# A two-layer retention and state-space trunk on one core: a reserve ahead of transposes in TensorE's order, a longer planned time for running-sum transfers, and a sigmoid as ScalarE's warm-up

## The chip, the cores and the metric

The kernel runs on one core of one Trainium2 chip. The metric is the device time of one execution in microseconds (us). TensorE (PE; PEld is its weight load) multiplies, VectorE (DVE) and ScalarE (ACT) do elementwise work, GpSimd (POOL) does a few small powers and accumulating transfers, and SyncE (SP) issues nearly all transfers. Every engine works through its own instructions strictly in the order in which they are written, and waits where an operand is not there yet.

## The reference

Two layers of: RMS norm; one wide projection; a retention mixer of four heads with rotary queries and keys; a state-space mixer of four groups with a causal convolution; gates; an output projection; RMS norm; a SwiGLU FFN. Sequence 256 in two chunks of 128, width 1024, all in float32. The parts that matter here:

```python
def hybrid_mixer(h, w_in, ...):
    u = h @ w_in
    q, k, v, g_ret, z, xbc, dt, gate_ret, gate_ssd = jnp.split(u, ...)
    yr = retention(rotary(q), rotary(k) * RET_DK ** -0.5, v)
    yr = silu(g_ret) * (yr * rsqrt(mean(yr * yr) + EPS))
    o_ret = yr @ ret_out
    xs, bm, cm = jnp.split(silu(causal_dwconv(xbc, conv_w, conv_b)), ...)
    dtp = softplus(dt + dt_bias)
    ys = ssd_scan(xs * dtp, dtp * a, bm, cm) + d_skip * xs   # exp(acs_i - acs_j), acs = cumsum(dtp * a)
    ys = ys * silu(z);  ys = ys * rsqrt(mean over a group(ys * ys) + EPS) * ssd_norm_w
    o_ssd = ys @ ssd_out
    return (sigmoid(gate_ret) * o_ret + sigmoid(gate_ssd) * o_ssd) @ w_o

def swiglu(h, w_gate_up, w_down):
    gate, up = jnp.split(h @ w_gate_up, [D_FF], axis=-1)
    return (silu(gate) * up) @ w_down
```

## The kernel before

A matrix product is done in three passes in a reduced float32 format: each operand is split into a high part (ACT, line 498 for the weights: `wh`) and the rest (DVE, line 519: `wl`), and lines 535 to 537 multiply high by high, high by low and low by high. Lines 954, 955 and 957 are the same for products whose weights stand still in PE (`fm_job`). A weight tile of 512 KB (`raw`) is loaded by SP (line 480) into one of 4 buffers and split into one of 6 pairs of `wh`, `wl`.

Work runs in jobs, one per block of columns: in the mixer v, gr and bc, then q, k and xs by turns, then g with the rest of xs, the product with `ret_out`, z, the product with `ssd_out`, and `w_o`; then the FFN. What comes out of a job with the sequence in rows must be turned for the next product. `transposed` (line 623; the transposes are line 630) does so: it takes a PSUM buffer `tr` (there are two), four PE transposes against the identity `ident` (part of the tile `cst`) fill it, ACT copies the high part and DVE subtracts for the low part. It is used on the gated retention (`g_post`), the gated state-space output (`z_post`), the gated FFN halves (`up_post`), the norms (`Norm.half`) and the merged mixer output (`ssd_post`). `xs_post` has transposes of its own (line 1505): the convolved, silu'd `sT` is turned back to rows.

The order of every engine's instructions is made in Python when the kernel is built. `Flow` plays the whole program as streams of operations, each with an engine, a planned cost in ns and a priority; whenever an engine is free in this play, it takes the ready operation of the lowest priority number and writes its instruction. A stream that yields a number waits for so many ns of planned time: no instruction comes of it, but what follows is written later on its engine. A transfer is waited for by such a number too. `Flow._loads` adds 1283 to an ACT operation whose function needs another table than the last one, but only when a last one is known: `self.table` begins as `None`.

`ssd_chunk` builds the decay matrix of one group and chunk. SP brings running sums broadcast to all partitions (line 1570, `seg<-acs`, 512 KB, two buffers `seg`); then ACT does eight 128-column differences (line 1580), then one 1024-column Exp, DVE multiplies it by the scores (`cbm`), and PE multiplies (`yps`, line 1612; `ips`, line 1599). The play gives the transfer 1500 for its issue on SP and 2500 after it.

At the start, `warm` runs one tiny ACT operation (line 1956) so that a function table is loaded before the data is there.

Of the kernel before, what the change touches and what calls it, by code (L numbers as in the profile page):

```python
# [11 lines left out]
AF = mybir.ActivationFunctionType  # L12
# [180 lines left out]
def trunk_kernel(  # L193
# [5 lines left out]
    nc = tc.nc  # L199
    HB, RB, TAIL, WARM = 6, 4, 5, 2  # L200
    APART, LATE = (), 2500.0
    PR0, SLACK = 1.6, 2500.0
    BESIDE = (8, 10, 12, 14, 11, 11, 9, 24, 44)
    APARTS, SUMS_PR = {}, 3.5
# [73 lines left out]
    mhalf = cp.tile([P, 2], F32, tag="mhalf", name="mhalf")  # L278
    junk = cp.tile([P, 2], F32, tag="junk", name="junk")
# [340 lines left out]
            for _ in range(4):  # L620
                fl.release(bigS["C"])

    def transposed(src, n, dst, i, t, pr, plain=None):
        yield from dst.take(i)
        yield trS

        def emit():
            ps = new_tr()
            for j in range(n):
                nc.tensor.transpose(out=ps[:, j * P : (j + 1) * P], in_=src[:, j * P : (j + 1) * P], identity=ident)  # L630
            return ps[:, : n * P].rearrange("p (j t) -> p j t", j=n)

        v = yield pe(110 * n, pr, emit)
        dh, dl = (a[:, :n, t * P : (t + 1) * P] for a in dst.at(i)[:2])
        yield act(n * P, pr, dh, v, AF.Copy, psum=True)
        yield tt(n * P, pr, dl, v, dh.bitcast(F32), ALU.subtract)
        fl.set(dst.ready[i][t])
        if plain:
            yield sxS
            x = new_sx("plain")  # L640
            yield act(n * P, pr, x.rearrange("p (j t) -> p j t", j=n), v, AF.Copy, psum=True)
            fl.set(plain, x)
        fl.release(trS)
# [545 lines left out]
    def layer(l, mix, nxt, opening=None):  # L1189
# [300 lines left out]
        def xs_post(g, jj):  # L1490
            def post(ps, second, j):
                if jj == 0:
                    yield bigS["C"]
                    fl.set(xs_t[g], new_big("C", F32, (P, NT, 512)))
                xs = yield xs_t[g]
                yield sxS
                sT = new_sx("sT").rearrange("p (b t) -> p b t", b=2)
                yield from conv(ps, second, 4 * g + 2 * jj, sT, j)
                yield trS

                def emit():
                    tps = new_tr()
                    for t in range(NT):
                        for b in range(2):
                            nc.tensor.transpose(out=tps[:, (2 * t + b) * P : (2 * t + b + 1) * P],  # L1505
                                                in_=sT[:, b, t * P : (t + 1) * P], identity=ident)
                    return tps

                tps = yield pe(440, j, emit)
                yield act(512, j, xs[:, :, jj * 256 : (jj + 1) * 256], tps.rearrange("p (t c) -> p t c", t=NT),  # L1510
                          AF.Copy, psum=True)
                fl.release(sxS)
                fl.release(trS)
                fl.set(xs_ev[g][jj])
            return post
# [48 lines left out]
        def ssd_chunk(g, t, lp, pr, dtt, acs, dec, dr, prm, cb, xs, x0_ev):  # L1564

            yield segS

            def bring():
                sg = new_seg()
                nc.sync.dma_start(out=sg, in_=dr[t, g * HPG : (g + 1) * HPG, :].partition_broadcast(P))  # L1570
                return sg

            sg = yield Op("sp", 1500, bring, lp)
            yield 2500.0
            c0 = t * NH + g * HPG

            def differences():

                for i in range(HPG):
                    nc.scalar.activation(out=sg[:, i, :], in_=sg[:, i, :], func=AF.Relu, scale=-1.0,  # L1580
                                         bias=acs[:, c0 + i : c0 + i + 1])

            yield Op("act", HPG * (0.833 * P + 185), differences, lp)
            yield act(1024, lp, sg, sg, AF.Exp, scale=-1.0)
            yield tt(1024, lp, sg, sg, cb[:, 2 * t, :].unsqueeze(1).broadcast_to([P, HPG, P]), ALU.mult)
            yield sxS
            xdt = new_sx("xdt")
            yield tt(512, lp, h3(xdt), h3(xs[:, t, :]), hb(dtt, t * NH, g), ALU.mult)
            yield sxS
            tail = new_sx("tail")  # L1590
            dsb = prm[:, 2, g * HPG : (g + 1) * HPG].unsqueeze(2).broadcast_to([P, HPG, HD])
            yield tt(512, lp, h3(tail), h3(xs[:, t, :]), dsb, ALU.mult)
            if t == 1:
                x0 = yield x0_ev
                yield accS

                def inter():
                    ps = new_acc("ips")
                    nc.tensor.matmul(ps, lhsT=cb[:, 1, :], rhs=x0, start=True, stop=True)  # L1599
                    return ps  # L1600

                ips = yield pe(856, pr, inter)
                yield tt(512, lp, h3(x0), h3(ips), hb(dec, 0, g), ALU.mult)
                fl.release(accS)
                yield tt(512, lp, tail, tail, x0, ALU.add)
                fl.release(sxS)
            yield accS

            def intra():
                ps = new_acc("yps")  # L1610
                for i in range(HPG):
                    nc.tensor.matmul(ps[:, i * HD : (i + 1) * HD], lhsT=sg[:, i, :], rhs=xdt[:, i * HD : (i + 1) * HD],  # L1612
                                     start=True, stop=True)
                return ps

            yps = yield pe(1780, pr, intra)
            fl.release(segS)
            yield tt(512, lp, xs[:, t, :], yps, tail, ALU.add)
            fl.release(accS)
            fl.release(sxS)  # L1620
            if t == 0:
                yield tt(512, lp, h3(xdt), h3(xdt), hb(dec, NH, g), ALU.mult)
                fl.set(x0_ev, xdt)
            else:
                fl.release(sxS)
                fl.release(cbmS)
                fl.set(ys_ev[g])
# [9 lines left out]
        yr = Operand(RH, ["Y", "Y", "A", "A"])  # L1637

        def g_post(hd):
            def post(t, ps, j, sem):  # L1640
                yield silS
                sil = new_sil()
                yield act(512, j, sil, ps, AF.Silu, psum=sem is accS)
                fl.release(sem)
                yt, rs = yield ret_ev[hd]
                yield stt(512, j, sil, yt[:, t, :], rs[:, t : t + 1], sil, ALU.mult, ALU.mult)
                if t == 1:
                    fl.release(bigS["A"])
                yield from transposed(sil, 4, yr, hd, t, j)
                fl.release(silS)  # L1650
            return post

# [15 lines left out]
        yz = Operand(SG, ["Y", "Y", "C", "C"])  # L1668
# [8 lines left out]
        def z_post(g):  # L1677
            def post(t, ps, j, sem):
                yield silS
                sil = new_sil()  # L1680
                yield act(512, j, sil, ps, AF.Silu, psum=sem is accS)
                fl.release(sem)
                yield ys_ev[g]
                y = xs_t[g].value[:, t, :]
                yield tt(512, j, sil, sil, y, ALU.mult)
                ss, ms = small2("ss"), small2("ms")
                yield act(512, j, y, sil, AF.Square, accum_out=ss[:, :1])
                if t == 1:
                    fl.release(bigS["C"])
                yield ts(1, j, ms[:, :1], ss[:, :1], 1.0 / 512, EPS, ALU.mult, ALU.add)  # L1690
                rz = yield from power(ms, 1, j, "rz", 6)
                w = yield wbs[g // 2]
                yield stt(512, j, sil, sil, rz[:, :1], w[:, (g % 2) * 512 : (g % 2 + 1) * 512], ALU.mult, ALU.mult)
                wb_left[g // 2] -= 1
                if not wb_left[g // 2]:
                    fl.release(wbS)
                yield from transposed(sil, 4, yz, g, t, j)
                fl.release(silS)
            return post

# [92 lines left out]
        def up_post(sg_ev, c):  # L1793
            def post(t, ps, j, sem):
                s = yield sg_ev[t]
                yield tt(512, j, s, ps, s, ALU.mult)
                fl.release(sem)
                yield from transposed(s, 4, gu, c, t, j)
                fl.release(silS)
            return post  # L1800

# [113 lines left out]
    def whole():  # L1915
# [37 lines left out]
        yield dve(8, -2, fills)  # L1953

        def warm():
            yield Op("act", 1400, lambda: nc.scalar.activation(out=junk, in_=mhalf, func=AF.Copy), -3)

        fl.spawn(warm())
        fl.spawn(warm_pe())
# [102 lines left out]
```

## Time and profile before

| what | us |
|---|---|
| median of 3 runs (1268.36 to 1273.1) | 1272.93 |
| the profiled execution | 1270.24 |
| its span, first to last instruction | 1268.4 |
| PE busy | 1254.4 |
| DVE busy | 1016.1 |
| ACT busy | 831.9 |
| granted TensorE clock, mean | 0.999 |

All times in rows are from the span's start. Matmuls are pipelined, so two that follow each other overlap: what one costs is read from the distance between two starts, not from its length. A stall of PE is the distance between two starts beyond what the same pair takes where nothing is late. Rows in brackets show idle time and who ended it.

### The profile page before, as it was taken

The page shows a single profiled execution, that of the slowest core. Times are in us where ns is not written, and L with a number is a line of the kernel's source. Part 1 is how long each engine was busy: PE and PEld are TensorE (multiplying, and loading weights), DVE is VectorE, ACT ScalarE, POOL GpSimd, SP SyncE. Part 2 cuts the span into 40 slices and gives each one's busy share as a digit, 9 for nine tenths or more (in the row PEclk, how much of TensorE's full clock was granted, in tenths as well). Part 3 has the DMA queues.
Part 4 walks back from the last instruction along what each step waited for, and adds up shares of the span by engine and source line. Part 5 has one row for each costly group of instructions (what it writes and reads, how often), then busy time and mean ns, then how long its engine had stood idle before and what let it go on. Part 6 is the DMA issues. An engine that isn't in the chain of part 4 may idle for free.

```text
span 1268.4 us, 17450 instructions
## 1 busy us (share of the span) xinstructions
PE 1254.4 (99%) x6330; PEld 1059.5 (84%) x6330; DVE 1016.1 (80%) x1388; ACT 831.9 (66%) x1244; POOL 52.3 (4%) x76
## 2 busy tenths in 40 slices
PE   9999999999999999999999999999999999999997
PEld 7789888888888888888888898888788888788886
DVE  6998888878576678999788888878875756889996
ACT  6876786786365466776576676866854643766754
POOL 0000000000010001001000000000000000010010
PEclk9999999999999999999999999999999999999999
DMA  8668554555565457886676475555555564678863
GB/s 297 219 167 285 181 174 166 175 182 192 158 222 201 159 175 223 291 223 210 225 218 219 126 263 167 167 183 181 186 181 171 203 207 150 210 205 266 287 175 119
DMA packets 72455, 253.96 MB, mean 200 GB/s; under 512 B 8336, under 2 KB 8592, under 8 KB 72368
## 3 DMA queue, kind: packets, MB, share of 16 engines
q1 hardware_dynamic: 66832, 233.32, 54.4%
q0 software_dynamic: 5248, 18.99, 7.7%
q8 instruction: 50, 0.82, 0.3%
q10 hardware_dynamic: 288, 0.52, 0.1%
q14 instruction: 37, 0.30, 0.1%
HBM read 251.69 MB, written 1.11 MB: 199 GB/s over the span
## 4 chain that ended last, share of the span: by engine, by line
PE 87%; ACT 5%; DMA 3%; DVE 2%; issue 2%; SPq 0%; POOLq 0%; POOL 0%; ACTq 0%
PE acc L535 19%; PE acc L536 19%; PE acc L537 19%; PE acc L954 13%; PE acc L955 8%; PE tr L630 2%; PE yps L1612 2%; PE acc L957 2%; ACT wh L498 1%; DMA seg<-acs 1%; DVE wl L519 1%; DMA raw<-in_w_tm_dram 1%; ACT seg L1580 1%; PE ips L1599 1%; PE tr L1505 1%
## 5 line engine op out<-in xcount | busy, mean ns | idle before, releaser
L519 DVE TENSOR_TENSOR wl<-raw,wh 128x1024 fp32r<-128x1024 f32 (+2 forms) x400 | 474.9, 1197 | 124.1 <-ACT wh L498 122.5
L498 ACT ACTIVATE wh<-raw 128x1024 fp32r<-128x1024 f32 (+2 forms) x400 | 409.1, 1036 | 207.4 <-PE acc L537 106.4
L954 PE MATMUL acc<-xT,wh 128*128 128x512 f32 x840 | 304.8, 400 | 0.0
L955 PE MATMUL acc<-xT,wl 128*128 128x256 f32 x960 | 250.8, 281 | 0.0
L535 PE MATMUL acc<-wh,xT 128*128 128x512 f32 (+1 forms) x568 | 219.7, 387 | 0.0
L537 PE MATMUL acc<-wh,xT 128*128 128x512 f32 (+1 forms) x568 | 216.3, 381 | 0.0
L536 PE MATMUL acc<-wl,xT 128*128 128x512 f32 (+1 forms) x568 | 216.2, 381 | 0.0
L955 PEld LDWEIGHTS acc<-xT,wl 128*128 128x128 f32 x960 | 181.6, 189 | 10.3
L954 PEld LDWEIGHTS acc<-xT,wh 128*128 128x128 f32 x840 | 158.1, 188 | 31.7
L537 PEld LDWEIGHTS acc<-wh,xT 128*128 128x128 f32 x568 | 106.7, 188 | 19.5
L536 PEld LDWEIGHTS acc<-wl,xT 128*128 128x128 f32 x568 | 106.8, 188 | 19.4 <-issue 0.5
L535 PEld LDWEIGHTS acc<-wh,xT 128*128 128x128 f32 x568 | 106.8, 188 | 18.9 <-issue 0.9
L498 ACT ACTIVATE wh<-raws 128x1024 fp32r<-128x1024 f32 x64 | 67.3, 1057 | 30.6 <-DVE raws L227 14.9
L519 DVE TENSOR_TENSOR wl<-raws,wh 128x1024 fp32r<-128x1024 f32 x64 | 77.3, 1221 | 8.7 <-ACT wh L498 7.9
L535 PE MATMUL acc<-wh,A 128*128 128x512 f32 x192 | 76.4, 398 | 0.0
L230 DVE SCALAR_TENSOR_TENSOR cc<-cc,cv 128x255 f32<-128x255 f32 (+1 forms) x144 | 68.4, 479 | 9.4 <-ACT cc L220 8.5
L537 PE MATMUL acc<-wh,A 128*128 128x512 f32 x192 | 74.9, 390 | 0.0
L536 PE MATMUL acc<-wl,A 128*128 128x512 f32 x192 | 74.8, 390 | 0.0
L535 PE MATMUL acc<-wh,C 128*128 128x512 f32 (+1 forms) x184 | 72.3, 393 | 0.0
L536 PE MATMUL acc<-wl,C 128*128 128x512 f32 (+1 forms) x184 | 71.1, 387 | 0.3
L537 PE MATMUL acc<-wh,C 128*128 128x512 f32 (+1 forms) x184 | 70.8, 385 | 0.0
L535 PE MATMUL acc<-wh,Y 128*128 128x512 f32 x160 | 64.5, 403 | 0.0
(176 smaller groups left out, 1850.4 us busy)
## 6 DMA issues: line engine op xcount, KB each, us to landing
raw<-in_w_tm_dram SPq DMA_DIRECT2D x104, 512.0 KB, 4.3
raw<-in_w_fm_dram SPq DMA_DIRECT2D x80, 512.0 KB, 4.2
raw<-in_w_gf_dram SPq DMA_DIRECT2D x40, 512.0 KB, 4.8
raw<-in_ret_out_dram SPq DMA_DIRECT2D x32, 512.0 KB, 4.1
raw<-in_ssd_out_dram SPq DMA_DIRECT2D x32, 512.0 KB, 3.3
raw<-in_w_gate_up_dram SPq DMA_DIRECT2D x32, 512.0 KB, 5.1
raw<-in_w_down_dram SPq DMA_DIRECT2D x28, 512.0 KB, 4.3
raw<-in_w_gr_dram SPq DMA_DIRECT2D x24, 352.0 KB, 4.1
```

Source lines behind the costliest of these rows:

```text
L230: return Op("dve", 1.04 * n + 130, lambda: nc.vector.scalar_tensor_tensor(out=out, in0=in0, scalar=scalar, in1=in1, op0=op0, op1=op1), pr)
L498: nc.scalar.activation(out=wh[:, :m], in_=raw[:, :m], func=AF.Copy)
L519: nc.vector.tensor_tensor(out=wl[:, :m], in0=raw[:, :m], in1=wh[:, :m].bitcast(F32), op=ALU.subtract)
L535: nc.tensor.matmul(ps, lhsT=lh, rhs=rh, start=first, stop=False, **kw)
L536: nc.tensor.matmul(ps, lhsT=lh, rhs=rl, start=False, stop=False, **kw)
L537: nc.tensor.matmul(ps, lhsT=ll, rhs=rh, start=False, stop=last, **kw)
L630: nc.tensor.transpose(out=ps[:, j * P : (j + 1) * P], in_=src[:, j * P : (j + 1) * P], identity=ident)
L954: nc.tensor.matmul(a, lhsT=wh[:, k % 4, fsl], rhs=x[:, k % 4, :, :], start=k == 0, stop=False)
L955: nc.tensor.matmul(a[:, :SEQ], lhsT=wl[:, k % 4, fsl], rhs=xh[:, k % 4, :], start=False, stop=False)
L957: nc.tensor.matmul(a, lhsT=wh[:, k % 4, fsl], rhs=x[:, k % 4, :, :], start=False, stop=True)
L1505: nc.tensor.transpose(out=tps[:, (2 * t + b) * P : (2 * t + b + 1) * P], in_=sT[:, b, t * P : (t + 1) * P], identity=ident)
L1612: nc.tensor.matmul(ps[:, i * HD : (i + 1) * HD], lhsT=sg[:, i, :], rhs=xdt[:, i * HD : (i + 1) * HD], start=True, stop=True)
```

## The change

Four things are written anew. `transposed` takes a `slack`: having got its PSUM buffer, the stream waits that long in planned time before its transposes become ready; `g_post`, `z_post` and `up_post` pass 1500, the norms and `ssd_post` pass none. `xs_post` waits 1500 likewise. The planned time behind the issue of a running-sum transfer goes from 2500 to 5000, so 6500 with the issue. The warm-up operation is a Sigmoid instead of a Copy, and the play is told so, so the first table is known to it. Nothing that is computed changes, and each engine has the same instructions but for table loads. Lines of the changed kernel stand 1 to 4 further down (498 is 499, 630 is 633, 1505 is 1509, 1580 is 1584).

```diff
+    SLOW = 1500.0
...
-    def transposed(src, n, dst, i, t, pr, plain=None):
+    def transposed(src, n, dst, i, t, pr, plain=None, slack=0.0):
         yield from dst.take(i)
         yield trS
+        if slack:
+            yield slack
...
                 yield from conv(ps, second, 4 * g + 2 * jj, sT, j)
                 yield trS
+                yield SLOW
...
             sg = yield Op("sp", 1500, bring, lp)
-            yield 2500.0
+            yield 5000.0
...
-                yield from transposed(sil, 4, yr, hd, t, j)
+                yield from transposed(sil, 4, yr, hd, t, j, slack=SLOW)
...
-                yield from transposed(sil, 4, yz, g, t, j)
+                yield from transposed(sil, 4, yz, g, t, j, slack=SLOW)
...
-                yield from transposed(s, 4, gu, c, t, j)
+                yield from transposed(s, 4, gu, c, t, j, slack=SLOW)
...
-            yield Op("act", 1400, lambda: nc.scalar.activation(out=junk, in_=mhalf, func=AF.Copy), -3)
+            yield Op("act", 1400, lambda: nc.scalar.activation(out=junk, in_=mhalf, func=AF.Sigmoid), -3, "sigmoid")
```

Three places show what this does to the order. First, ACT in the opening of layer 0: `D<-acc,rstd` is the first sigmoid (of the gate columns), `sil,ss<-h` the sum of squares of half a row of x, `xT` and `plain` what the transposes leave. Before:

```order
L498 ACTIVATE wh<-raw 128x1024
L220 ACT_TABLE_LOAD
L220 ACTIVATE D<-acc,rstd 128x320
L220 ACTIVATE xT<-tr 128x4x128
L498 ACTIVATE wh<-raw 128x1024
L220 ACTIVATE plain<-tr 128x512 x2
L498 ACTIVATE wh<-raw 128x1024
L220 ACTIVATE sil,ss<-h_79 128x512
```

and in the change:

```order
L499 ACTIVATE wh<-raw 128x1024
L221 ACTIVATE D<-acc,rstd 128x320
L221 ACTIVATE xT<-tr 128x4x128
L499 ACTIVATE wh<-raw 128x1024
L221 ACTIVATE plain<-tr 128x512 x2
L499 ACTIVATE wh<-raw 128x1024
L221 ACTIVATE sil,ss<-h_79 128x512
```

The table load is gone; the rest stands as it stood. Over the whole program ACT has 33 table loads before and 34 in the change: this one fewer and, in the mixer of layer 0 and elsewhere, two more.

Second, ACT in layer 1, where group 2's running sums are used while xs of group 3 is convolved: `seg<-seg,acs` are the differences, `seg<-seg` the Exp, `sT<-cc` the silu whose result PE then transposes. Before, from the table load for the Exp to that silu:

```order
L220 ACT_TABLE_LOAD
L220 ACTIVATE seg<-seg 128x1024
L220 ACTIVATE cc<-acc 128x256
L220 ACTIVATE cc<-cc,cv 128x256
L498 ACTIVATE wh<-raw 128x1024 x2
L220 ACTIVATE cc<-cc,cv 128x256
L498 ACTIVATE wh<-raw 128x1024
L220 ACTIVATE seg<-seg 128x1024
L220 ACTIVATE cc<-acc 128x256
L498 ACTIVATE wh<-raw 128x1024
L220 ACT_TABLE_LOAD
L220 ACTIVATE sT<-cc 128x512
```

and in the change, from the second set of differences:

```order
L1584 ACTIVATE seg<-seg,acs 128x128 x8
L221 ACTIVATE sT<-cc 128x512
L221 ACTIVATE cc<-cc,cv 128x256
L499 ACTIVATE wh<-raw 128x1024 x3
L221 ACTIVATE C<-tr 128x2x256
L221 ACTIVATE cc<-acc 128x256
L221 ACT_TABLE_LOAD
L221 ACTIVATE seg<-seg 128x1024
```

The silu now stands before both Exp operations and needs no table load of its own; on PE the four transposes of its result moved 24 matmuls towards the front.

Third, PE in layer 1's FFN, at the transposes of the first gated pair. Before, both halves stand together:

```order
L954 MATMUL acc<-xT,wh 128x512
L955 MATMUL acc<-xT,wl 128x256
L630 MATMUL tr<-cst,sil 128x128 x8
L954 MATMUL acc<-xT,wh 128x512
L955 MATMUL acc<-xT,wl 128x256
L954 MATMUL acc<-xT,wh 128x512
L955 MATMUL acc<-xT,wl 128x256
L954 MATMUL acc<-xT,wh 128x512
L955 MATMUL acc<-xT,wl 128x256 x2
L957 MATMUL acc<-xT,wh 128x512
```

and in the change:

```order
L957 MATMUL acc<-xT,wh 128x512
L958 MATMUL acc<-xT,wl 128x256
L957 MATMUL acc<-xT,wh 128x512
L958 MATMUL acc<-xT,wl 128x256
L957 MATMUL acc<-xT,wh 128x512
L958 MATMUL acc<-xT,wl 128x256
L633 MATMUL tr<-cst,sil 128x128 x4
L958 MATMUL acc<-xT,wl 128x256
L960 MATMUL acc<-xT,wh 128x512
L633 MATMUL tr<-cst,sil 128x128 x4
```

The first four stand three pairs of matmuls later (the three pairs that came right behind them before), the second four two matmuls behind those. Outside the mixers of both layers, such shifts are all that changes on PE; inside them, from the second xs transposes to the product with `ret_out`, retention products, transposes and `yps`, `ips` change places.

## The prediction

> **What bounds the kernel now.** I read the page first, then the waits of PE, then the timeline and the chain of waits around each place where PE stood still. The page's busy times, and PE's waits (us in all, times, longest):
>
> ```profile
> PE 1254.4 (99%) x6330; PEld 1059.5 (84%) x6330; DVE 1016.1 (80%) x1388; ACT 831.9 (66%) x1244; POOL 52.3 (4%) x76
> ```
>
> ```profile
> PE tr L1505 <- ACT sT L220: 2.8, 3, 1.6
> PE tr L630 <- DVE sil L230: 1.4, 1, 1.4
> PE idle L1945 <- DVE mhalf L1922: 1.3, 1, 1.3
> PE tr L630 <- DVE sil L227: 1.1, 1, 1.1
> ```
>
> PE is the bound, and there is little idle time to win: four kinds of wait, 6.6 us in all, half a per cent of the span. Three of the four are transposes (L630, L1505) whose source ACT or DVE had not finished; the fourth is the start. PE works in order, so everything behind a transpose waits as well. No change of order can win much more than these; the question is how much of the transposes' part goes.
>
> The stalls, read as the distance between starts, in order of time. The group at 566 also gives what is normal: a 256-column pass (L955) holds PE for 0.12, a 512-column one for 0.23.
>
> ```profile
> 35.04 0.39 PE L537 MATMUL acc<-wh,C 128*128 128x512 f32 x1
> 36.86 0.63 PE L630 MATMUL tr<-cst,sil 128*128 128x128 f32 x4 [1.43 <-DVE sil L230]
> ...
> 282.59 0.39 PE L537 MATMUL acc<-wh,xT 128*128 128x512 f32 x1
> 283.92 0.33 PE L1505 MATMUL tr<-cst,sT 128*128 128x128 f32 x1 [0.94 <-ACT sT L220]
> ...
> 565.99 0.28 PE L955 MATMUL acc<-xT,wl 128*128 128x256 f32 x1
> 566.11 0.40 PE L954 MATMUL acc<-xT,wh 128*128 128x512 f32 x1
> 566.34 0.28 PE L955 MATMUL acc<-xT,wl 128*128 128x256 f32 x1
> 566.65 0.33 PE L630 MATMUL tr<-cst,sil 128*128 128x128 f32 x1
> ...
> 818.68 0.28 PE L955 MATMUL acc<-xT,wl 128*128 128x256 f32 x1
> 819.21 0.33 PE L1505 MATMUL tr<-cst,sT 128*128 128x128 f32 x1 [0.25 <-ACT sT L220]
> ...
> 908.02 0.39 PE L537 MATMUL acc<-wh,xT 128*128 128x512 f32 x1
> 909.98 0.44 PE L1505 MATMUL tr<-cst,sT 128*128 128x128 f32 x2 [1.56 <-ACT sT L220]
> ...
> 1105.95 0.28 PE L955 MATMUL acc<-xT,wl 128*128 128x256 f32 x1
> 1107.31 1.25 PE L630 MATMUL tr<-cst,sil 128*128 128x128 f32 x8 [1.08 <-DVE sil L227]
> ```
>
> So the stalls are 1.59 (at 35), 1.10 (at 283), 0.19 (566), 0.41 (819), 1.73 (909) and 1.24 (1107), together 6.26 us.
>
> **The change part by part.**
>
> *The sigmoid warm-up* takes a table load off ACT. The stall at 35 lies behind it. ACT's timeline, SP's, and from the page what a weight tile of that kind takes to land (median, us):
>
> ```profile
> 27.90 1.28 ACT L220 ACT_TABLE_LOAD   x1
> 29.19 0.53 ACT L220 ACTIVATE D<-acc,rstd 128x320 f32<-128x320 f32 x1
> ...
> 33.56 2.02 ACT L498 ACTIVATE wh<-raw 128x1024 fp32r<-128x1024 f32 x2
> ```
>
> ```profile
> 27.12 2.37 SPq L480 DMA_DIRECT2D raw<-in_w_fm_dram  x2
> ```
>
> ```profile
> raw<-in_w_fm_dram SPq DMA_DIRECT2D x80, 512.0 KB, 4.2
> ```
>
> From 27.90 on ACT has no idle row until these two `wh` are done; DVE's `wl` and then the `sil` that PE wants stand behind them. Without the load all of it moves up by 1.28. What could hold it is a weight tile that has not landed: the second `wh` began near 34.5 and would begin at 33.2; its tile is the second of the two issues, some 2 us after 27.12, so 29.2 + 4.2 = 33.4. So 1.0 to 1.28 is won, and I take 1.2; 0.3 to 0.4 of the stall stays. The operation at the start loads one table in both kernels, so nothing is paid there. [...]
>
> *The 6.5 us for the running sums* is behind the three stalls at L1505. The chain of waits ahead of the longest, and of the tile `seg` ACT's wait for these transfers (us, times) and their time from issue to landing:
>
> ```profile
> 884.24 6.38 DMA seg<-acs
> 890.64 2.46 ACT seg L1580 x8
> ...
> 909.29 0.64 ACT sT L220
> ```
>
> ```profile
>   DMA seg<-acs: 8.4, 6
> ...
> DMA to landing us min/median/max: 3.8/5.1/7.2
> ```
>
> The play allowed 4.0, the transfers took 5.1 in the median. ACT stood 8.4 us in 6 places, with all its later work behind it, and the silu `sT` was late for PE. At 6.5 planned, only a transfer near the longest, 7.2, is late, by 0.7, and the transposes have 1.5 in hand. In layer 1 the silu now even stands ahead of both Exps and two table loads (2 x 1.28), while its transposes moved up by 24 matmuls, 24 x 0.23 = 5.5 at most: the one about pays for the other, and what is left of the stall is ACT's lateness, which the longer plan takes away. I take all three as gone: 1.10 + 0.41 + 1.73 = 3.24. Bounds: 1.51, if the longest stays whole where its transposes moved up, and 3.24.
>
> *The reserve of 1.5 us* moves L630 back. At 1107 three pairs go ahead, 3 x (0.23 + 0.12) = 1.05, so 0.19 of 1.24 stays. The 0.19 at 566 goes, with eight more matmuls ahead of its transposes. Sum 1.24; lower bound 1.05.
>
> *What it costs.* The transposes' results come 1.5 later. Behind the last z group stands the product with `ssd_out`, which reads that group in its last five of 16 steps at the earliest; the eleven before are 11 x 12 passes of 0.23, 30 us of cover. Were it gone, each would cost its 1.5. Two `tr` buffers are held longer; nothing on PE is queued for them but other transposes. ACT gets two more table loads, 2.6 us, hidden by the 34% of the span in which it is idle; exposed, they would cost that.
>
> The order of both mixers is made anew, and a new order can have a late operand of its own. Nearest row, of the waits of PE's weight loads:
>
> ```profile
> PEld acc L536 <- DVE wl L519: 2.9, 7, 0.5
> ```
>
> Outside transposes lateness reaches 0.5 at a time, with one longest of 1.73 among the transposes. Between none (a new order may as well have fewer) and two of the longest, 3.5, I take 0.5, since with the reserve the same lateness must pass 1.5 before PE sees it.
>
> Sum: 1.2 + 3.24 + 1.24 - 0.5 = 5.2 us, bounds 0.1 (1.0 + 1.51 + 1.05 - 3.5) and 5.8 (1.28 + 3.24 + 1.24). The profiled execution, 1270.24 (its span and 1.84 around it), becomes 1265.0. It lies 2.7 below the median of the three runs; the middle of all four is 1271.6, and from there it is 1266.4. I say 1266.
>
> **The rivals.**
>
> *The waits move rather than go.* Each late operand comes back at another place of the new mixer order, and only the warm-up and the FFN's shift pay: 1.2 + 1.24 = 2.4, time 1269. For it: only the running sums get a longer plan, and the tiles of `raw`, which had their share in the 1107 stall, do not. Against it: no such wait above 0.5 shows at present outside transposes.
>
> *More than the sum.* The three runs spread over 4.7 us, and the profiled one is below their median. If the slower runs differ by later transfers, the same transposes catch it there, and a reserve of 1.5 takes that away too: 8 us from the median, 1265. For it: the spread is of the stalls' size. Against it: nothing shows where the slow runs lose.
>
> *Slower.* SP works in order, and the last two `seg` loads of a layer wait for a buffer that PE frees (L1612), with weight tiles queued behind them:
>
> ```profile
> SPq L1570 <- PE yps L1612: 7.8, 4, 3.3
> ```
>
> The longer plan puts `yps` later. A tile of `ret_out` feeds 12 passes, 2.7 us; 4 raw and 6 split tiles are 27 us of reserve at most. Say half is filled: the wait must go from 3.3 to over 13 before PE starves, and it costs what is beyond. At 20 in both layers that is 2 x 7 = 14, less 5.2: slower by 9, 1280. Against it: 3 tiles stand behind the last load as before, and the loads moved by a place or two.
>
> *The transfers land in time anyway.* [...] With transfers inside the old 4.0 the 3.24 falls away and 2.0 is left, 1270. The shortest of the 16 took 3.8 and ACT did wait 8.4, so this is as good as excluded.
>
> **How the numbers follow.** My forecast (4.3 to 6.3 won, 1265.3 to 1267.3 from the middle run): 0.60. Moved waits: 0.23. More than the sum: 0.13. Slower: 0.03. In time anyway: 0.01. The forecast alone ranges from 1263 to 1268, by the run that it is taken from; with the moved waits above and the larger gain below, 1261 to 1271 leaves out the slower case and the two ends. What a measurement here can tell from no change is about 0.5%, 6.4 us: faster by that means under 1266.6, from the median. That is two thirds of my forecast (0.40) and most of the larger gain (0.11), together 0.51; slower 0.03; within 0.46.
>
> **What would show it.** Right: no table load before the first sigmoid, and the third group of transposes at some 35.6 with an idle of 0.2; ACT's wait for `seg` under 2 us in all; PE's wait for `sT` gone; the FFN transposes of layer 1 with 0.2 or none. Wrong: new rows of PE or PEld waiting in the mixers, ACT still idle for `seg`, or a wait of SP for `yps` above 10. A span that falls by 5 while the runs' median does not move would mean that the runs differ by something outside these stalls.

## The result, and the profile after

The changed kernel takes 1262.91 us in the median of 6 runs (1261.89 to 1263.68); the kernel before, run beside it, 1273.01 (1268.36 to 1276.12). The ratio is 0.9924, with a 95% interval of 0.9902 to 0.9946: faster by 10.1 us, where 1266 had been said. A second set of 6 runs gave 1262.75 against 1273.07. The profiled execution took 1261.89, its span 1260.1, which is 8.3 less than the span before. The times of the runs also lie closer together: within 1.8 us, before within 7.8.

The page of the changed kernel, its busy times and the head of its chain of waits, and its list of PE's waits (us in all, times, longest), which has these two rows and no other:

```profile
PE 1251.6 (99%) x6330; PEld 1061.8 (84%) x6330; DVE 1017.9 (81%) x1388; ACT 832.7 (66%) x1245; POOL 52.6 (4%) x76
...
PE 95%; DVE 2%; DMA 1%; issue 1%; ACT 0%; POOLq 0%; POOL 0%; ACTq 0%
```

```profile
PE idle L1949 <- DVE mhalf L1926: 1.3, 1, 1.3
PE acc L537 <- DVE wl L520: 0.2, 1, 0.2
```

All waits of transposes are gone. PE's idle time, span less busy, fell from 14.0 to 8.5 us, and its busy time by 2.8 with the same 6330 instructions. The idle rows ahead of the six stalls were 5.26 of that, while the stalls, read from start to start, were 6.26: the last matmul ahead of a stall still runs for 0.16 (0.39 less 0.23), which counts as busy. That is 1.0 of the 2.8; the other 1.8 lies in small spacings that no row of waits shows, so the six stalls were not all that was late.

The three places in the order of the program. First the opening, on ACT and on PE:

```profile
26.51 1.05 ACT L499 ACTIVATE wh<-raw 128x1024 fp32r<-128x1024 f32 x1
27.46 0.51 ACT L221 ACTIVATE D<-acc,rstd 128x320 f32<-128x320 f32 x1
...
33.16 1.06 ACT L499 ACTIVATE wh<-raw 128x1024 fp32r<-128x1024 f32 x1 [0.27 <-DMA raw<-in_w_fm_dram]
```

```profile
34.68 0.39 PE L538 MATMUL acc<-wh,C 128*128 128x512 f32 x1
35.11 0.63 PE L633 MATMUL tr<-cst,sil 128*128 128x128 f32 x4
```

No table load ahead of the sigmoid; the second weight tile is now waited for, 0.27; the transposes start 0.43 behind the last pass instead of 0.23, a stall of 0.20 where there was 1.59. Second, layer 1, where the longest stall was (ACT, then PE):

```profile
893.08 2.45 ACT L1584 ACTIVATE seg<-seg,acs 128x128 f32<-128x128 f32 x8
895.43 0.62 ACT L221 ACTIVATE sT<-cc 128x512 f32<-128x512 f32 x1
```

```profile
897.82 0.39 PE L538 MATMUL acc<-wh,xT 128*128 128x512 f32 x1
898.05 0.60 PE L1509 MATMUL tr<-cst,sT 128*128 128x128 f32 x4
```

The differences start without a wait, the silu follows, and its result is there 2.0 us before PE comes for it (895.43 + 0.62 against 898.05). Before, the transposes started 0.05 behind the end of their silu, having waited for it. Third, the FFN of layer 1:

```profile
1100.30 0.28 PE L958 MATMUL acc<-xT,wl 128*128 128x256 f32 x1
1100.42 0.60 PE L633 MATMUL tr<-cst,sil 128*128 128x128 f32 x4
```

0.12 between the starts, which is what a 256-column pass holds PE for: no stall. ACT has no wait for `seg` left at all, and its transfers took 4.2/5.0/5.6 us (shortest, median, longest), all inside the planned 6.5.

### The profile page after: what moved, and what is told of

It is laid out like the page before. It is cut to its first block, busy times and chain, and to the rows that moved or that the text cites. A ratio compares the mean times of both kernels' runs of the same rounds, so it can differ in the third digit from the quotient of the medians.

```text
span 1260.1 us, 17460 instructions
## 1 busy us (share of the span) xinstructions
PE 1251.6 (99%) x6330; PEld 1061.8 (84%) x6330; DVE 1017.9 (81%) x1388; ACT 832.7 (66%) x1245; POOL 52.6 (4%) x76
## 4 chain that ended last, share of the span: by engine, by line
PE 95%; DVE 2%; DMA 1%; issue 1%; ACT 0%; POOLq 0%; POOL 0%; ACTq 0%
PE acc L536 20%; PE acc L537 20%; PE acc L538 20%; PE acc L957 16%; PE acc L958 9%; PE tr L633 2%; PE acc L960 2%; PE yps L1616 2%; DVE wl L520 1%; DMA raw<-in_w_dw_dram 1%; PE tr L1509 1%; PE acc L1376 1%; PE ips L1603 1%; PE idle L1949 0%; PE y L537 0%
```

## The experiments

Twelve experiments ran, in three sets that each had their own runs of the kernel before beside them (medians 1272.43, 1273.07 and 1272.44). Only the second, from "changed, again" to reserve_3000, also had the changed kernel beside it; for late_silu and reserve_all the difference to the changed kernel is taken from its first 1262.91, and is good to the 0.6 by which the medians of before differ. In the table "ACT for `seg`" is the time that ACT waited for the running sums in the profiled execution, and "L1505" the longest wait of PE for `sT` there.

| kernel | median (range), us | runs | ratio to before, 95% | ACT for `seg` | L1505 |
|---|---|---|---|---|---|
| before, again | 1272.71 (1270.48–1274.34) | 8 | 0.9996 [0.9982, 1.0010] | 9.6 | 2.5 |
| warm_only | 1272.45 (1268.84–1276.42) | 12 | 0.9998 [0.9983, 1.0013] | 10.5 | 1.9 |
| seg_only | 1267.48 (1266.11–1270.97) | 9 | 0.9956 [0.9942, 0.9971] | 0.2 | none |
| reserve_only | 1264.67 (1263.44–1266.44) | 6 | 0.9934 [0.9918, 0.9950] | 2.2 | none |
| xs_reserve_only | 1266.88 (1265.42–1268.24) | 8 | 0.9950 [0.9932, 0.9967] | 4.9 | none |
| l630_reserve_only | 1266.27 (1265.54–1267.24) | 7 | 0.9951 [0.9931, 0.9971] | 4.6 | 0.2 |
| changed, again | 1262.75 (1262.05–1263.70) | 6 | 0.9921 [0.9901, 0.9942] | none | none |
| no_warm | 1264.04 (1263.70–1265.32) | 6 | 0.9933 [0.9909, 0.9956] | none | none |
| no_seg | 1264.06 (1262.65–1264.42) | 6 | 0.9930 [0.9909, 0.9951] | 2.0 | none |
| reserve_3000 | 1262.90 (1262.56–1263.38) | 6 | 0.9922 [0.9902, 0.9943] | 2.0 | none |
| late_silu | 1268.22 (1266.51–1269.68) | 10 | 0.9964 [0.9949, 0.9979] | none | 3.2 |
| reserve_all | 1264.97 (1264.13–1265.73) | 6 | 0.9938 [0.9915, 0.9962] | none | none |

### The kernel before again: what differs between its runs

No edit; it gives a second trace of the same program.

> The kernel before, unchanged: a second profiled execution of it. Its six times so far spread from 1268.36 to 1276.12, those of the change from 1261.89 to 1263.68. Theory 'lateness at the transposes': where this execution is slower than the first profiled one (span 1268.4), the extra stands as longer PE waits at the same places (tr L1505 from ACT sT, tr L630 from DVE sil), 1 to 3 us each; where it is as fast, the places and sizes are those of the first profile within 0.3 us. Rival 'something else': a slower span with the same transposes' stalls, and the extra in matmul spacing, in the opening or in waits for weight tiles.

The median is that of before. ACT's waits for the running sums and PE's waits for the silu, of the first profiled execution (PE's two rows, 0.94 and 1.56, stand in the prediction):

```profile
264.59 2.46 ACT L1580 ACTIVATE seg<-seg,acs 128x128 f32<-128x128 f32 x8 [1.02 <-DMA seg<-acs]
890.64 2.46 ACT L1580 ACTIVATE seg<-seg,acs 128x128 f32<-128x128 f32 x8 [1.63 <-DMA seg<-acs]
```

and of the second, ACT and then PE:

```profile
266.18 2.45 ACT L1580 ACTIVATE seg<-seg,acs 128x128 f32<-128x128 f32 x8 [2.53 <-DMA seg<-acs]
893.88 2.46 ACT L1580 ACTIVATE seg<-seg,acs 128x128 f32<-128x128 f32 x8 [1.30 <-DMA seg<-acs]
```

```profile
282.68 0.39 PE L537 MATMUL acc<-wh,xT 128*128 128x512 f32 x1
285.51 0.87 PE L1505 MATMUL tr<-cst,sT 128*128 128x128 f32 x4 [2.45 <-ACT sT L220]
286.03 0.77 PE L535 MATMUL acc<-wh,xT 128*128 128x512 f32 x1
286.61 0.63 PE L536 MATMUL acc<-wl,xT 128*128 128x512 f32 x1
287.03 0.63 PE L537 MATMUL acc<-wh,xT 128*128 128x512 f32 x1
...
913.22 0.66 PE L1505 MATMUL tr<-cst,sT 128*128 128x128 f32 x4 [1.23 <-ACT sT L220]
```

ACT waits 1.02, 1.63, 2.53, 1.30; some 19 us later PE waits 0.94, 1.56, 2.45, 1.23. It is the same wait, handed on nearly whole: less 0.07 or 0.08 each time. Between the two ACT does not rest, so it cannot catch up. The windows of the first and of the second execution (length, then busy us of PE, PEld, DVE, ACT):

```profile
264.60:283.90 19.30, 18.38 (x94) 15.31 (x92) 14.08 (x23) 19.22 (x37) 0.00 (x0) 1.00 0.50 167
```

```profile
266.20:285.50 19.30, 16.86 (x85) 13.99 (x83) 13.85 (x22) 19.21 (x37) 0.00 (x0) 1.00 0.42 145
```

ACT is busy for 19.2 of 19.3 us there, although it is idle for a third of the span as a whole. ACT's other waits for `seg` did not reach PE like this: the longest of the first execution, 2.54 at 302, has no wait of PE behind it, and 0.70 at 799 came out as 0.25. So the time of a run of before depends on when a few of these transfers land. The first profiled execution had landed well at the first place (1.02); the second waited 2.53 there, and more followed: behind its stall passes start 0.43 apart instead of 0.23. Its windows around that place (the last columns are PEclk, DMA share, GB/s):

```profile
282.00:285.40 3.40, 1.06 (x5) 0.56 (x3) 3.40 (x5) 3.34 (x6) 0.00 (x0) 1.00 0.66 246
285.40:289.00 3.60, 3.49 (x11) 2.90 (x12) 3.59 (x6) 2.01 (x5) 0.00 (x0) 0.56 0.80 280
289.00:300.00 11.00, 11.00 (x63) 9.45 (x63) 9.41 (x12) 6.21 (x9) 0.00 (x0) 0.99 0.51 164
```

In the 3.6 us behind the stall the mean granted clock was 0.56. The eight passes there lose 8 x 0.20 = 1.6 on top of the 2.60 of the stall. The second span is 2.9 longer than the first (1271.3 against 1268.4), and this one place accounts for it: 1.50 more of stall, as the theory had it, and 1.6 in the spacing of matmuls, where the rival had looked. Other runs of before fit this: of the 57 beside the experiments, the 21 with a mean granted clock of 0.996 or 0.997 have a median of 1274.6, the 22 with 0.999 one of 1271.2.

### Each part alone: warm_only, seg_only, reserve_only

```diff
warm_only     AF.Copy  ->  AF.Sigmoid, ..., "sigmoid"      (L1956)
seg_only      yield 2500.0  ->  yield 5000.0               (L1574)
reserve_only  + yield SLOW in xs_post; slack=SLOW in g_post, z_post, up_post
```

> Only the warm-up operation is a sigmoid; the order of every engine stays as before but for one table load less on ACT. By the prediction's sum: 1.2 us less (1.0 to 1.28), the PE stall at 35 us falls from 1.6 to 0.3, all other stalls as before; times as widely spread as before's (over 4 us). [...] If the spread of the times came from the opening, it would fall here to under 2 us.

> Only the planned time of the running-sum transfers is 6.5 instead of 4.0 us; no reserve, warm-up as before. Prediction: ACT's wait for seg falls from 8.4 to under 2 us and the three stalls at L1505 (3.2 us) mostly go, the FFN stall of 1.2 and that at 35 (1.6) stay: 1.5 to 3.2 us less in the profile. Theory 'ACT's wait for the running sums makes the spread': the times spread under 2 us and the median falls by 6 or more. Theory 'zero reserve at the transposes makes the spread': they still spread over 3 us and the median falls by 1 to 4.

> Only the 1.5 us reserve ahead of the transposes of xs, gated retention, gated state-space output and FFN; running sums planned at 4.0 as before, warm-up as before. Prediction: ACT still waits some 8 us for seg, the FFN stall falls to 0.2, the L1505 stalls lose up to 1.5 each: 2.5 to 4 us less in the profile. Theory 'zero reserve makes the spread': the times spread under 2.5 us and the median falls by 6 or more. Theory 'ACT's wait makes the spread': spread over 3 us, median 2 to 4 less.

The warm-up alone wins nothing that shows in the median: the stall at 35 is gone from its trace (in an opening in which a weight tile had come late before it, so this trace does not decide whether the 0.3 expected would have been left), but the rest of the order is that of before, and its runs lie 7.6 us apart. Two of ACT's seven waits for `seg`, 1.95 and 1.93 of 10.5 us in all, came out as stalls of 2.04 and 2.01 at the same two places.

The longer plan alone wins 5.0, the reserve alone 7.8, more than the terms of 3.24 and 1.24 that they stood for. Together with nothing for the warm-up they would make 12.8, and the change won 10.1: seg_only and reserve_only take away the same stalls at L1505. Under the reserve ACT still waits 2.2 us for `seg`, but PE does not notice.

Neither theory of the spread came out whole. With the longer plan alone the runs still lie 4.9 apart, although no stall at L1505 is left: in its trace PE waits at L630, 1.5, 1.3 and 0.9 us. That trace is also of the slowest of its nine runs, with a span of 1269.1, 0.7 more than before where 1.5 to 3.2 less had been expected. With the reserve alone the runs lie 3.0 apart, closer to what "zero reserve makes the spread" had said (under 2.5), and the span is 3.7 less, as expected.

### Each part undone: no_warm, no_seg; and twice the reserve

```diff
no_warm       the changed kernel with  AF.Copy  for the warm-up
no_seg        the changed kernel with  yield 2500.0
reserve_3000  the changed kernel with  SLOW = 3000.0
```

> The changed kernel, unchanged, once more and beside the runs that leave one part out. 1262.9 with a spread of about 2 us, as before; the profile with no PE wait over 0.5 us behind the opening.

> The change without the sigmoid warm-up: one more table load on ACT ahead of the first sigmoid, every other instruction in the changed kernel's order. Alone, the warm-up moved the median by nothing (1272.45 against 1272.43, interval from -2.2 to +1.7 us), lost in the spread; here the spread is small. Prediction's term: 1.2 us slower than the changed kernel, with a stall of 1.3 to 1.6 at the third group of transposes (near 36 us). Rival, the opening is limited by transfers whatever ACT does: within 0.4 us of the changed kernel.

> The change with the running sums planned at 4.0 us as before. By the prediction's own terms the longer plan carried most of the three stalls: 2 to 3 us slower than the changed kernel, ACT waiting some 8 us for seg. Theory 'the reserve of 1.5 alone suffices': within 0.7 us of the changed kernel, ACT's wait for seg back at 8 us, and no PE wait behind it.

> The reserve at 3.0 instead of 1.5 us of planned time, everything else as changed. If the reserve costs nothing because what reads the transposes has cover (prediction), within 0.6 us of the changed kernel, a little less if lateness beyond 1.5 still occurred. If holding the two PSUM buffers longer costs (rival), slower by 1 us or more, with new waits of PE or ACT around the transposes. ACT has 6 more table loads here (7.7 us): if ACT's time mattered, it would show as well.

The changed kernel came again as expected, its longest wait of PE 0.4 us. Without the sigmoid the stall at the opening is back, on ACT and on PE:

```profile
27.61 1.28 ACT L221 ACT_TABLE_LOAD   x1
28.91 0.53 ACT L221 ACTIVATE D<-acc,rstd 128x320 f32<-128x320 f32 x1
```

```profile
34.94 0.39 PE L538 MATMUL acc<-wh,C 128*128 128x512 f32 x1
36.57 0.63 PE L633 MATMUL tr<-cst,sil 128*128 128x128 f32 x4 [1.25 <-DVE sil L231]
```

1.63 - 0.23 = 1.40 of stall against 0.20 in the changed kernel, 1.2; in the medians 1.3.

Without the longer plan the medians are 1.3 apart as well, but no stall at L1505 stands behind it: ACT waits 2.0 us for `seg`, and the reserve covers it. Both expectations had this wait at some 8 us; it is 2.2 in reserve_only too, so the order that the reserve makes leaves little of it by itself. PE's weight loads wait as long for the splits without the plan as in the second execution with it (in the first it was 2.0):

```profile
PEld acc L537 <- DVE wl L520: 4.1, 9, 0.9
```

```profile
PEld acc L537 <- DVE wl L520: 4.0, 9, 0.9
```

Most of the difference between the traces lies in the opening. By 40 us, before any running sum is loaded, no_seg is 1.1 us behind the first profiled execution of the changed kernel and 0.9 behind the second; at the end it is 2.3 and 1.1 behind (a span of 1262.4 against 1260.1 and 1261.3). And the two sets of runs overlap (1262.65 to 1264.42, 1262.05 to 1263.70). So behind the reserve the longer plan is worth between nothing and 1.3, and which is not settled.

Twice the reserve is as fast as the reserve of 1.5 (1262.90), with six table loads more on ACT than the changed kernel: holding the transposes back costs nothing that shows, and 1.5 was already enough.

### Which transposes: xs_reserve_only and l630_reserve_only

```diff
xs_reserve_only    the kernel before, + yield SLOW in xs_post alone
l630_reserve_only  the kernel before, slack=SLOW in g_post, z_post, up_post alone
```

> The kernel before with the reserve of 1.5 us in xs_post alone (the transposes at L1505), everything else as before. Theory: it is the silu sT of the mixers that comes late by a different amount in each run, so this part carries most of what the whole reserve won alone (7.8 us): about 5 us, 1267.5, the stalls at L1505 under 0.4 us each, and the times of the runs closer together (within 3.5 us instead of 8). Rival: the gain is that of the other transposes (L630); then under 2.5 us are won here and the runs stay as far apart as before.

> The kernel before with the reserve of 1.5 us for the transposes of g_post, z_post and up_post alone (L630), xs_post as before. Theory: only the stalls of the gated FFN halves and their like go, 1.2 to 2 us, 1271, with the stalls of 1 to 2.6 us at L1505 still there and the runs as far apart as before (about 8 us). Rival: this part carries most of the 7.8 us of the whole reserve, 5 or more.

The first came as expected (5.6 won, runs within 2.8 us, nothing left at L1505). The second did not: 6.2 won, and the runs within 1.7 us. My theory that only the reserve ahead of L1505 can take the spread away fell. In the trace of l630_reserve_only, ACT and PE at the place where before ACT had waited 1.02 and PE 0.94:

```profile
265.56 2.43 ACT L1583 ACTIVATE seg<-seg,acs 128x128 f32<-128x128 f32 x8
...
279.56 1.28 ACT L221 ACT_TABLE_LOAD   x1 [0.53 <-DVE cc L231]
280.85 0.63 ACT L221 ACTIVATE sT<-cc 128x512 f32<-128x512 f32 x1
```

```profile
281.88 0.60 PE L1508 MATMUL tr<-cst,sT 128*128 128x128 f32 x4
```

Held-back transposes elsewhere changed the order of the whole mixer: in this execution the running sums have landed before the differences are due, and ahead of the silu ACT has even 0.53 to spare. Of ACT's remaining waits for `seg` in that kernel, 4.6 us, one of 0.94 comes out as a wait of PE, of 0.16; the others do not reach PE. The long stalls at L1505 belonged to one order, in which a wait had no slack behind it; three different edits each left it. That the sums land in time in every run of this kernel is not shown, as it has one trace; that its runs lie within 1.7 us speaks for it.

### A late silu on purpose: late_silu

```diff
     the changed kernel, in conv, which xs_post calls
-            yield act(512, pr, dst, cvt, AF.Silu)
+            silu = act(512, pr, dst, cvt, AF.Silu)
+            if l == 1 and blk == 12:
+                once = silu.fn
+                silu.fn = lambda: [once() for _ in range(9)]
+            yield silu
```

> The changed kernel with one silu sT of layer 1's mixer (a block of group 3, first chunk) written nine times on ACT instead of once: eight more operations of about 0.63 us, 5 us that the planner does not know of, and the order as in the changed kernel. PE's transposes of it come some 5 us late, less the reserve of 1.5 and what else was in hand: a stall of 2 to 4 us at one place. Theory (a stall of about 2 us or more is followed by a stretch at half the TensorE clock): right behind it a stretch of 3 to 4 us in which matmuls start every 0.43 us instead of 0.23 and a granted clock near 0.55, so the cost is the stall and about 1.5 us more, 4 to 5.5 us against the changed kernel. Rival: the cost is the stall alone, 2 to 4 us, the spacing stays 0.23 and the clock 1.00.

The block is the first pair of channel blocks of group 3. ACT, PE and the windows of its profiled execution:

```profile
896.92 5.91 ACT L221 ACTIVATE sT<-cc 128x512 f32<-128x512 f32 x9
```

```profile
899.30 0.39 PE L538 MATMUL acc<-wh,xT 128*128 128x512 f32 x1
902.89 1.11 PE L1513 MATMUL tr<-cst,sT 128*128 128x128 f32 x4 [3.20 <-ACT sT L221]
903.65 0.77 PE L536 MATMUL acc<-wh,xT 128*128 128x512 f32 x1
...
908.49 0.58 PE L538 MATMUL acc<-wh,xT 128*128 128x512 f32 x1
908.91 0.39 PE L536 MATMUL acc<-wh,xT 128*128 128x512 f32 x1
```

```profile
903.60:909.20 5.60, 5.60 (x16) 4.40 (x15) 4.89 (x7) 5.57 (x8) 0.00 (x0) 0.53 0.36 112
909.20:914.00 4.80, 4.80 (x23) 3.96 (x22) 4.68 (x7) 4.34 (x6) 0.00 (x0) 1.00 0.68 240
```

A stall of 3.59 - 0.23 = 3.36, then twelve passes in 5.26 us (903.65 to 908.91) instead of 12 x 0.23 = 2.76, and four transposes that hold PE for 0.76, in the changed kernel 0.35. That is 3.36 + 2.50 + 0.41 = 6.3; the medians are 5.3 apart (1268.22 - 1262.91). In this execution the stall alone does not make the loss: the stretch at half clock is real, and somewhat longer than the 3 to 4 us expected. How much of the 5.3 it makes in the median stays open: the mean granted clock of the ten runs goes from 0.996 to 0.999, where the changed kernel has 0.998 or 0.999, and the two with 0.999 took 1267.76 and 1268.07. The silu was 5.91 - 0.62 = 5.29 us late; the 2.0 that it has in hand in the changed kernel took the other 1.9.

### The reserve everywhere: reserve_all

```diff
     the changed kernel
+    slack=SLOW in Norm.half and in ssd_post too
```

> The changed kernel with the reserve of 1.5 us in the norms (Norm.half) and in ssd_post too. What is left of stalls at transposes in the changed kernel is 0.2 us at 35 and small ones in the opening. If the reserve costs nothing anywhere: 0 to 0.5 us faster than the changed kernel, 1262.5. Rival: the norms have no other work for PE to put ahead of their transposes, so there the reserve only holds back what PE needs next: 1 to 3 us slower than the changed kernel, 1264 to 1266.

The rival was right: 2.1 slower than the changed kernel (1264.97 against 1262.91), or 1.0 to 2.2 by the spans of the profiled executions (1262.3 against 1261.3 and 1260.1). On PE in the opening, where the norm's transposes now start late:

```profile
38.29 0.40 PE L538 MATMUL acc<-wh,C 128*128 128x512 f32 x1
39.56 0.50 PE L957 MATMUL acc<-xT,wh 128*128 128x512 f32 x1 [0.87 <-DVE xT L228]
```

The next product needs what the norm's transposes leave, and there is no other work to put ahead: 1.27 - 0.23 = 1.04 lost here; the only other waits of PE in that trace are two of 0.2 for what the norms leave, so the rest of the 2.1 is not placed. No kernel ran faster than the changed one; the one with twice the reserve is as fast.

## Why the prediction was right, and where its sizes were off

**What bounds the kernel.** Right. PE's stalls at transposes were what could be won, and they went: of 6.26 there is 0.20 left, at 35. The whole gain against the first profiled execution, 8.3, is 2.2 more than that; these are small delays that the list of stalls did not have, and they are not placed.

**The time.** 1266 was said and 1262.91 came, just under the 1263 to which the forecast alone reached and inside the whole range of 1261 to 1271. The way and the places were right, the gain from the median was too small by a third (6.9 against 10.1), for the reasons below.

***The sigmoid warm-up.*** Right: 1.2 said, 1.2 in the trace and 1.3 in the medians when undone. The second weight tile does become the limit, as worked out, with 0.2 of stall left instead of 0.3 to 0.4. Where the load comes back, in no_warm, it starts at 27.61 and takes 1.28, and the sigmoid starts at 28.91, 0.02 behind its end.

***The 6.5 us for the running sums.*** The mechanism is right: ACT's wait for these transfers was PE's wait for the silu, to 0.08 us. The size is where the sum fell short. The 3.24 was read from one execution, in which the transfers happened to land early at 283; in the two other traces of that order the stall there was 2.60 and 2.04, each with a stretch at half clock behind it (mean granted clock 0.56 over 3.6 us in before_again, 0.52 over 3.3 in warm_only) that the prediction did not have. And the term is not the plan's own: the reserve alone removes the same stalls. Worth 5.0 alone, the plan is worth at most 1.3 on top of the reserve.

***The reserve of 1.5 us.*** Its own 1.24, the stalls at L630 in the FFN, went as said. But the prediction let it count at L630 only; it also keeps lateness at L1505 from PE, and moves the mixer into an order in which that lateness is smaller. Alone it is worth 7.8, the largest part.

***What it costs.*** Nothing that shows, where 0.5 had been taken. No new wait of PE above 0.2 came (0.4 in the second trace of the changed kernel), the reserve of 3.0 costs no more, and SP's wait for `yps` did not grow:

```profile
SPq L1574 <- PE yps L1616: 6.0, 2, 3.3
```

**The rivals.** "More than the sum", given 0.13, is what happened in kind: where the slower runs have a trace they lose at these same transposes, and the change takes the spread away, from 7.8 us to 1.8. Its price, 8 us from the median, was nearer to the 10.1 measured than the forecast's. "Nothing shows where the slow runs lose" was true of one trace; a second trace of the unchanged kernel showed it at once. "The waits move rather than go" is excluded by the changed kernel's waits, "Slower" by SP's, and "The transfers land in time anyway" by ACT's 9.6 us for `seg` in the second trace of before; the shortest of these transfers in any trace took 3.6 (l630_reserve_only), and the medians of the traces lie at 4.7 to 5.5, beyond the 4.0 that the play had allowed.

**The base.** The prediction set its sum of 5.2 against a middle run of 1271.6. From the profiled execution, 5.2 was said and 8.3 came: 0.5 for costs that did not arise, 0.4 since the stalls went more fully than the terms had it (6.06 against 5.68), and the 2.2 that are not placed. From the median 10.1 came: that execution was a quick one of before by 2.7 us, while the changed kernel has hardly a slow one. In the second trace of before what it was quick by stands at a place that the change mends; for the other runs it is likely, but not shown.

Open remains how the gain between medians splits by place, since only three executions of the old order have a trace.

## What to carry to other kernels

If an engine is full and another one feeds it in order, read how much time lies between the feeder's result and its use: 0.05 us, as at the late silus here, hands a late transfer on nearly whole, and a reserve of 1.5 in the planned order costs nothing that shows where other work can go ahead, and 1 to 2 us where none can. Where runs of a kernel spread over more than the gain in question, take a second trace of the unchanged kernel before pricing stalls, since one execution shows one draw of its late transfers. Parts that cure the same stall do not add: here 0, 5.0 and 7.8 alone made 10.1 together.

## What the runs showed of the hardware that I had not expected

Behind some stalls of TensorE of 2 us and more its granted clock was about half: behind 2.60 us in before_again (mean PEclk 0.56 over 3.6 us) and behind 3.36 in late_silu (0.53 over 5.6). Not behind every stall of 2.0: in warm_only two of the same kind and length, by PE's starts, went different ways.

```profile
284.47 0.39 PE L537 MATMUL acc<-wh,xT 128*128 128x512 f32 x1
286.74 0.66 PE L1505 MATMUL tr<-cst,sT 128*128 128x128 f32 x4 [1.87 <-ACT sT L220]
...
914.12 0.39 PE L537 MATMUL acc<-wh,xT 128*128 128x512 f32 x1
916.36 0.66 PE L1505 MATMUL tr<-cst,sT 128*128 128x128 f32 x4 [1.85 <-ACT sT L220]
```

A window behind the first and one behind the second (length, busy us of PE, and so on to PEclk):

```profile
288.00:291.30 3.30, 3.30 (x10) 2.60 (x9) 3.02 (x6) 1.98 (x5) 0.00 (x0) 0.52 0.90 286
...
917.00:921.00 4.00, 4.00 (x20) 3.26 (x19) 4.00 (x7) 3.70 (x6) 0.00 (x0) 1.00 0.85 282
```

Behind the first stall, 2.04 with 1.87 of it idle, eight passes start 0.43 apart, and the mean granted clock is 0.52; behind the second, 2.01 with 1.85 idle, passes start 0.23 apart at a clock of 1.00. In the opening of warm_only PE was idle for 1.38 ahead of its start at 20.85 and for 0.50 ahead of that at 21.78, and from 21.5 to 25.2 the clock was 0.55. In the first profiled execution of before, the stall of 1.73 at 909, 1.56 of it idle, left the clock at 1.00 from 910 to 914. What decides between the two cases no run shows. For a kernel that keeps PE full it means that a stall of some 2 us can cost 1.6 beyond its own length, 8 x 0.20 here as in before_again, and behind the 3.36 of late_silu it was 2.9 (2.50 + 0.41).
